# Half of a token's expert rows added by TensorE through diagonal weights, with the shared expert's down product in the same PSUM banks

## The chip, the core and the metric

The kernel runs on one core of one Trainium2 chip. The metric is the time of one execution on the device, in microseconds (us). The core has five engines that run their own instruction streams and meet at semaphores: TensorE (PE in the profile, its weight loads PEld), VectorE (DVE), ScalarE (ACT), GpSimd (POOL) and SyncE (SP). Transfers are issued by SyncE, ScalarE and GpSimd and run on 16 shared DMA engines.

## The reference, cut to what matters

The whole block is an adaptive norm, sparse attention and an RWKV7 branch side by side, their mix added to `x`, and then a mixture of experts. The change touches what follows the experts. With `T` = 512 tokens, `D` = 1024, 64 experts of width 256 and 8 experts for each token:

```
h2 = rms_norm(x, norm2_g) * (1 + sc2) + sh2
y[t] = sum over the 8 chosen experts e of  gw[t, e] * swiglu(h2[t], exp_gate[e], exp_up[e], exp_down[e])
shared = swiglu(h2, sh_gate, sh_up, sh_down)
x = x + g2 * (y + shared)
out = rms_norm(x, final_g)          # x * rsqrt(mean(x * x) + 1e-6) * final_g
```

All of it is float32.

## The kernel before

Tokens lie in four blocks `b` of 128 (one for each partition), so `x[b]` is a 128x1024 tile. The program has these stages, by the times of the profiled execution: the norms, attention and RWKV7 until about 680; the second norm, the router and the shared expert until about 808; the routed experts until about 1311; the end until 1388.

The shared expert. `shared_load` (L993) loads its weights, and GpSimd multiplies the down weights `shd` by `g2`. `shared_up` (L1006) makes `act`, the 256x512 product of gate and up. `shared_down` (L1020) is called for each block: two halves of 512 columns, two products each (`pssd`, L1027), and VectorE adds the result to `x[b]` (L1028).

The lists. `lists` (L1154) and `table` (L1177) turn the routing into a list of tokens for each expert: VectorE makes 32 one-hot masks `oh` (L1186), TensorE sums them against the tokens into `pstab` (L1188), VectorE copies that out (L1193) and forms rows `lr` (L1197), TensorE turns them (`psidx`, L1198) and VectorE casts them to the indices `idx` (L1199). `token_weights` (L1201) makes the weights `wk` of a token's eight rows. In this part a scheduler interleaves the instructions of the calls.

The routed experts. 50 slots of one expert each pass through six weight buffers `W[0]` to `W[5]` (3 MB each; `load_slot`, L1228, on SyncE's queue). Their tokens are worked in chunks of 64 rows: GpSimd gathers the rows (`gather`, L1241), VectorE transposes them (`hT`, L1252), `gate_up` (L1255) makes the product `pg`, ScalarE and VectorE make `sg` and `t` from it (L1269, L1271), `turn` (L1274) transposes `t`, and `down` (L1283) multiplies with the down weights; the result `o` is scaled by `g2` and stored in the DRAM tensor `od`, one row for each token and expert. This order is written out by hand. Slot 5's buffer lies where the lists and the shared expert's tiles were, so its load waits for them.

The end. `finish_begin` (L1388) makes 12 places for rows out of the buffers `W[1]` and `W[2]`, and puts `final_g` and two output tiles `ys` into `W[3]`. `finish` (L1399) is the branch that runs when no expert has more rows than its slot holds. For each block GpSimd gathers eight rows of 1024 for each token from `od` (L1406), VectorE adds each with its weight to `x[b]` (L1408), ScalarE sums the squares (L1411), VectorE takes the mean (L1412) and the reciprocal root in nine small steps (`rsqrt`, L143 to L155), scales (L1414), and SyncE stores the block (L1415). The scheduler mixes the blocks.

Of the kernel before, what the change touches and what calls it, by code (L numbers as in the profile page):

```python
# [19 lines left out]
P = 128  # L20
# [17 lines left out]
FILL = (3, 2)  # L38

# [123 lines left out]
class Block:  # L163
# [829 lines left out]
    def shared_load(self):  # L993
# [25 lines left out]

    def shared_down(self, b, pool, tag, bufs):  # L1020

        nc = self.nc
# [365 lines left out]
    def finish_begin(self):  # L1388

        flat = []  # L1390
        for j in (1, 2, 3):
            gu, d = self.W[j]
            gu = gu.rearrange("p j k f -> p (j k f)")
            flat.append([gu[:, D * m:D * m + D] for m in range(4)] + [d[:, m] for m in range(2)])
        self.rows = flat[0] + flat[1]
        self.fg, self.ys = flat[2][0], flat[2][1:3]
        self.nc.sync.dma_start(self.fg, self.ins["final_g"].rearrange("(o d) -> o d", o=1).to_broadcast([P, D]))

    def finish(self, od):  # L1399

        nc, fp, fg = self.nc, self.ep, self.fg
        for b in range(NB):
            x = self.x[b]
            for k in range(8):
                row = self.rows[(8 * b + k) % len(self.rows)]
                nc.gpsimd.indirect_dma_start(out=row, out_offset=None, in_=od,  # L1406
                                             in_offset=bass.IndirectOffsetOnAxis(ap=self.at[:, 8 * b + k:8 * b + k + 1], axis=0))
                nc.vector.scalar_tensor_tensor(x, row, self.wk[:, b, k:k + 1], x, op0=ALU.mult, op1=ALU.add)  # L1408
            y = self.ys[b % 2]
            ss, m, r = (fp.tile([P, 1], F32, tag=nm, name=nm, bufs=2) for nm in ("ss3", "m3", "r3"))  # L1410
            nc.scalar.activation(y, x, AF.Square, accum_out=ss)  # L1411
            nc.vector.tensor_scalar(m, ss, 1.0 / D, 1e-6, op0=ALU.mult, op1=ALU.add)  # L1412
# [129 lines left out]
```

## Time and profile before

| | us |
|---|---|
| time before, median of 3 runs | 1378.23 |
| lowest, highest | 1373.99, 1381.51 |
| the profiled execution | 1390.25 |
| its span | 1388.0 |
| TensorE, VectorE, ScalarE, GpSimd busy | 1192.2, 741.5, 304.2, 499.1 |

The mean granted clock of TensorE was 0.923 in the profiled execution. The span runs from the first to the last instruction or transfer of the execution; the rows further down are all taken from it, with times from its start. A shape such as 128x512 is partitions by elements. One float32 matmul call shows as two passes, so `shared_down`'s 16 calls are 32 instructions. "Idle before" is how long the engine stood before an instruction, and the arrow names what it was released by.

### The profile page before, as it was taken

How to read it: one execution, taken by the hardware profiler on the slowest of the kernel's cores; microseconds unless marked ns; L12 is line 12 of the kernel's file. 1: busy time of each engine (PE TensorE's matmuls, PEld its weight loads, DVE VectorE, ACT ScalarE, POOL GpSimd, SP SyncE). 2: the span in 40 equal slices, each digit the busy share in tenths (PEclk: the TensorE clock that was granted, in tenths of full speed). 3: DMA queues.
4: the chain of work that ended last, by engine and by line, in shares of the span. 5: the costliest groups of instructions: out<-in, count | busy, mean ns of one | idle time of the engine just before them, and what ended most of it. 6: DMA issues, size and time to landing. Idle time of an engine off the chain costs nothing. (4 is left out here: it accounts for less than half of the span.)

```text
span 1388.0 us, 25689 instructions
## 1 busy us (share of the span) xinstructions
PE 1192.2 (86%) x10057; PEld 727.7 (52%) x10057; DVE 741.5 (53%) x1783; ACT 304.2 (22%) x700; POOL 499.1 (36%) x483
## 2 busy tenths in 40 slices
PE   4899888998888899978889969999999999999600
PEld 3566555666666665666768634444444444444200
DVE  5783258887798977655566822222222222222167
ACT  6432411111133476524312000000000000000000
POOL 1555424433244734253421143333233333331073
PEclk9899999988899999989899979999999999999755
DMA  9683564200025842364371776999899999999586
GB/s 312 202 257 64 99 174 98 51 29 29 28 76 159 252 122 77 113 229 160 107 254 46 304 302 210 346 413 412 316 379 397 396 389 399 401 406 412 206 294 251
DMA packets 149342, 318.29 MB, mean 229 GB/s; under 512 B 13839, under 2 KB 89322, under 8 KB 130396
## 3 DMA queue, kind: packets, MB, share of 16 engines
q1 hardware_dynamic: 109332, 241.64, 48.9%
q0 software_dynamic: 19584, 43.27, 9.4%
q10 hardware_dynamic: 20296, 31.65, 6.3%
q8 instruction: 81, 1.33, 0.4%
q14 instruction: 49, 0.40, 0.1%
HBM read 278.58 MB, written 41.08 MB: 230 GB/s over the span
## 5 line engine op out<-in xcount | busy, mean ns | idle before, releaser
L1265 PE MATMUL pg<-wgu,hT 128*64 128x256 f32 (+1 forms) x3424 | 331.5, 397 | 17.4 <-DVE hT L1252 6.9
L1245 POOL DMA_INDIRECT G<-h2d,idx x160 | 151.3, 946 | 320.5 <-DVE hT L1252 271.7
L1265 PEld LDWEIGHTS pg<-wgu,hT 128*64 128x64 f32 (+1 forms) x3424 | 171.3, 123 | 171.4 <-issue 71.0
L1271 DVE TENSOR_TENSOR t<-sg,pg 128x128 f32<-128x128 f32 x80 | 23.0, 287 | 324.3 <-ACT sg L1269 324.3
L344 POOL TENSOR_TENSOR wl<-w,wh 128x512 fp32r<-128x512 f32 (+1 forms) x94 | 129.0, 1386 | 150.2 <-ACT wh L343 148.2
L182 PE MATMUL psz<-hh,wh 128*128 128x512 f32 (+1 forms) x352 | 150.2, 427 | 6.6 <-ACT wh L343 6.6
L1292 PE MATMUL pd<-wd,a 128*64 128x512 f32 (+1 forms) x856 | 153.8, 600 | 2.0 <-ACT a L1280 2.0
L183 PE MATMUL psz<-hl,wh 128*128 128x512 f32 (+1 forms) x352 | 150.1, 426 | 0.0
L184 PE MATMUL psz<-hh,wl 128*128 128x512 f32 (+1 forms) x352 | 147.6, 419 | 1.2 <-POOL wl L344 1.2
L343 ACT CAST wh<-w 128x512 fp32r<-128x512 f32 (+1 forms) x94 | 55.7, 611 | 140.3 <-PE psz L183 104.1
L182 PEld LDWEIGHTS psz<-hh,wh 128*128 128x128 f32 (+1 forms) x352 | 69.8, 198 | 28.4 <-issue 7.1
L1280 ACT COPY a<-psa 128x128 f32<-128x128 f32 x80 | 21.2, 265 | 281.5 <-PE psa L1278 154.8
L1294 DVE TENSOR_TENSOR o<-pd,g2h 128x512 f32<-128x512 f32 x80 | 55.3, 692 | 47.1 <-PE pd L1292 45.4
L183 PEld LDWEIGHTS psz<-hl,wh 128*128 128x128 f32 (+1 forms) x352 | 69.8, 198 | 17.4 <-issue 4.2
L1292 PEld LDWEIGHTS pd<-wd,a 128*64 128x64 f32 (+1 forms) x856 | 39.4, 122 | 74.3 <-issue 66.7
L184 PEld LDWEIGHTS psz<-hh,wl 128*128 128x128 f32 (+1 forms) x352 | 69.3, 197 | 17.2 <-POOL wl L344 2.1
L1269 ACT ACTIVATE sg<-pg 128x128 f32<-128x128 f32 x80 | 22.2, 277 | 174.4 <-PE pg L1265 158.7
L1252 DVE STREAM_TRANSPOSE hT<-G 128x512 f32<-128x512 f32 x80 | 56.3, 704 | 3.6 <-DMA G<-h2d,idx 3.6
L579 DVE STREAM_TRANSPOSE bdx<-X 32x128 f32<-32x128 f32 x160 | 48.3, 302 | 2.9
L239 DVE SCALAR_TENSOR_TENSOR acc<-adaw,sc,acc 128x1024 f32<-128x1024 f32 x28 | 44.1, 1576 | 9.9 <-DMA adaw<-in_ada_w_dram 9.4
L1406 POOL DMA_INDIRECT wgu<-od,rowat x22 | 23.7, 1079 | 68.4 <-issue 65.1
L779 DVE SCALAR_TENSOR_TENSOR acc<-rel,iw,acc 128x256 f32<-128x256 f32 (+2 forms) x45 | 38.1, 846 | 10.4 <-ACT rel L774 7.8
(414 smaller groups left out, 1872.7 us busy)
## 6 DMA issues: line engine op xcount, KB each, us to landing
wgu<-in_exp_gate_dram SPq DMA_DIRECT2D x50, 1024.0 KB
wgu<-in_exp_up_dram SPq DMA_DIRECT2D x50, 1024.0 KB
wd<-in_exp_down_dram SPq DMA_DIRECT2D x50, 1024.0 KB
adaw<-in_ada_w_dram SPq DMA_DIRECT2D x48, 512.0 KB
w<-in_w_in_dram SPq DMA_DIRECT2D x46, 512.0 KB
od<-o ACTq DMA_DIRECT2D x160, 128.0 KB
x<-in_x_dram SPq DMA_DIRECT2D x8, 512.0 KB
zg<-zst ACTq DMA_DIRECT2D x16, 256.0 KB
```

The lines of the kernel that those rows point to most:

```text
L182: nc.tensor.matmul(ps, ah, bh, start=first, stop=False)
L183: nc.tensor.matmul(ps, ah, bl, start=False, stop=False)
L184: nc.tensor.matmul(ps, al, bh, start=False, stop=last)
L239: nc.vector.scalar_tensor_tensor(acc, w, self.sc[:, k:k + 1], acc, op0=ALU.mult, op1=ALU.add)
L343: nc.scalar.copy(wh[:, ks, :n], w[:, ks, :n])
L344: nc.gpsimd.tensor_sub(wl[:, ks, :n], w[:, ks, :n], wh[:, ks, :n].bitcast(F32))
L579: nc.vector.transpose(bdx[z, :, z], X[z])
L1245: self.nc.gpsimd.indirect_dma_start(out=G[:, x], out_offset=None, in_=self.h2d.rearrange("t (q c) -> (t q) c", q=4), in_offset=bass.Indire ...
L1252: self.nc.vector.transpose(hT.rearrange("p k (s i) -> p s k i", i=32), G.rearrange("p s (k i) -> p s k i", i=32))
L1265: nc.tensor.matmul(pg[at:at + n], hT[:, k, n * x:n * x + n], ws[x][0][:, :, k, m::2], start=k == 0, stop=k == 7, tile_position=(0, at))
L1292: nc.tensor.matmul(pd[at:at + n], a[:, k, n * x:n * x + n], ws[x][1][:, k, T * h:T * h + T], start=k == 0, stop=k == 1, tile_position=(0, at))
L1294: nc.vector.tensor_mul(o, pd, self.g2h)
```

## The change

1. `shared_down` goes. The scaled `shd` is stored to DRAM (`shd_d`) on GpSimd's queue as soon as it is made, and `act` (`act_d`) on ScalarE's queue after `shared_up`. `finish_begin` loads both again, into `W[2]`, on SyncE's queue behind the last slot's load.
2. There are 28 places for rows instead of 12, in `W[4]`, `W[5]`, part of `W[3]`, `W[0]` and `W[1]`.
3. Of a block's eight rows, VectorE adds the first four to `x[b]`. The last four are added by TensorE: for each there is a 128x128 diagonal matrix `dg` of the token weights (16 in all, made by ScalarE during the last chunks, in `W[3]`), and `dg` times the row is accumulated in PSUM. The same two PSUM banks of a block get `act` times `shd` (the shared down product) and the identity times `x[b]`, so that they hold the whole sum.
4. Square and scale read PSUM, in two halves of 512 columns; the two sums of squares are added by one small step more. The output is stored in eight halves.
5. The order of the end is written out by hand (`manual_schedule`).

The core of the diff:

```diff
@@ shared_load
+        nc.gpsimd.dma_start(self.shd_d, self.shd)
@@ shared_down
-    def shared_down(self, b, pool, tag, bufs):
-        for hf in range(2):
-            ds = slice(hf * T, hf * T + T)
-            ps = pool.tile([P, T], F32, tag=tag, name="pssd", bufs=bufs)
-            for k in range(2):
-                nc.tensor.matmul(ps, self.act[:, k, b * P:(b + 1) * P], self.shd[:, k, ds], start=k == 0, stop=k == 1)
-            nc.vector.tensor_add(self.x[b][:, ds], self.x[b][:, ds], ps)
@@ finish_begin
-        self.rows = flat[0] + flat[1]
+        self.rows = flat[4] + flat[5] + flat[3][2:] + flat[0] + flat[1]
+        self.act, self.shd = flat[2][3].rearrange("p (k t) -> p k t", k=2), self.W[2][1]
+        self.dg = [flat[3][j // 8][:, P * (j % 8):P * (j % 8) + P] for j in range(NB * PEROWS)]
+        nc.sync.dma_start(self.shd, self.shd_d)
+        nc.sync.dma_start(self.act, self.act_d)
+        for b in range(NB):
+            for j in range(PEROWS):
+                nc.scalar.activation(self.dg[PEROWS * b + j], self.ident, AF.Copy, scale=self.wk[:, b, 8 - PEROWS + j:9 - PEROWS + j])
@@ finish
+        def shared(b):
+            sums[b] = [self.ps.tile([P, T], F32, tag=t, bufs=3, name="pssd") for t in ("pg", "pd")]
+            for h, hs in enumerate(halves):
+                for k in range(2):
+                    nc.tensor.matmul(sums[b][h], self.act[:, k, b * P:(b + 1) * P], self.shd[:, k, hs], start=k == 0, stop=False)
+        def last(b):
+            for h, hs in enumerate(halves):
+                nc.scalar.activation(y[:, hs], sums[b][h], AF.Square, accum_out=ss[:, h:h + 1])
+            nc.vector.tensor_add(m, ss[:, 0:1], ss[:, 1:2])
+            nc.vector.tensor_scalar(m, m, 1.0 / D, 1e-6, op0=ALU.mult, op1=ALU.add)
+            rsqrt(nc, fp, m, r, 1, "r3u")
+            for h, hs in enumerate(halves):
+                nc.vector.scalar_tensor_tensor(y[:, hs], sums[b][h], r, fg[:, hs], op0=ALU.mult, op1=ALU.mult)
+                nc.sync.dma_start(self.out[0, b * P:(b + 1) * P, hs], y[:, hs])
+        with self.tc.manual_schedule():
+            for b in range(NB):
+                for k in range(8): nc.gpsimd.indirect_dma_start(out=place(b, k), ...)
+                if b == 0:
+                    for c in range(NB - 1): shared(c)
+                for k in range(n):
+                    add(b, k)
+                    if b and k == 1: last(b - 1)
+                if b == NB - 1: shared(b)
+                for h, hs in enumerate(halves):
+                    nc.tensor.matmul(sums[b][h], self.ident, self.x[b][:, hs], start=False, stop=False)
+                for j in range(PEROWS):
+                    for h, hs in enumerate(halves):
+                        nc.tensor.matmul(sums[b][h], self.dg[PEROWS * b + j], place(b, n + j)[:, hs], start=False, stop=j == PEROWS - 1)
+            last(NB - 1)
@@ build
         self.shared_up(1, self.ps, "pd", 3)
+        nc.scalar.dma_start(self.act_d, self.act)
         self.load_slot(4)
         self.lists()
-        for b in range(NB):
-            self.shared_down(b, self.ps, "pd", 3)
         self.token_weights()
```

How the instructions stand in a row shows at three places. The first is TensorE just before the experts: `pstab` is the one-hot product, `psidx` the turning of the index rows, `pg` the first chunk's gate and up product. Before:

```order
L1188 MATMUL pstab<-tok,oh 60x64
L1027 MATMUL pssd<-shd,act 128x512
L1188 LDWEIGHTS oh
L1188 MATMUL pstab<-tok,oh 128x64
L1188 LDWEIGHTS oh
L1188 MATMUL pstab<-tok,oh 60x64
L1027 MATMUL pssd<-shd,act 128x512 x3
L1198 MATMUL psidx_7763<-idl,lr 128x128
L1027 MATMUL pssd<-shd,act 128x512
L1198 MATMUL psidx_7763<-idl,lr 128x60
L1027 MATMUL pssd<-shd,act 128x512 x3
L1265 MATMUL pg<-wgu_7450,hT 64x256 x20
```

After (lines 1181, 1191, 1258, 1271 are 1188, 1198, 1265, 1278 of before):

```order
L1181 MATMUL pstab<-tok,oh 60x64
L1181 LDWEIGHTS oh
L1181 MATMUL pstab<-tok,oh 128x64
L1181 LDWEIGHTS oh
L1181 MATMUL pstab<-tok,oh 60x64
L1191 MATMUL psidx_7769<-idl,lr 128x128
L1191 MATMUL psidx_7769<-idl,lr 128x60
L1258 MATMUL pg<-wgu_7455,hT 64x256 x20
L1271 MATMUL psa<-idl,t 128x128
```

The `pssd` products between the one-hot products, between the two `psidx` and behind them are gone, and nothing takes their place.

The second is VectorE in the end; `x_6852` and `x_6960` are the sums of blocks 1 and 2, `m` and `r` the mean and the root of block 0. Before:

```order
L1408 SCALAR_TENSOR_TENSOR x_6852<-wgu_7454,wk,x_6852 128x1024 x2
L1412 TENSOR_SCALAR m_12853<-ss_12852 128x1
L146 TENSOR_SCALAR r3u<-m_12853 128x1
L147 TENSOR_SCALAR r_12854<-r3u 128x1
L1408 SCALAR_TENSOR_TENSOR x_6852<-wd_7455,wk,x_6852 128x1024
L151 SCALAR_TENSOR_TENSOR r3u<-r_12854,m_12853 128x1
L152 SCALAR_TENSOR_TENSOR r_12854<-r3u,r_12854 128x1
L151 SCALAR_TENSOR_TENSOR r3u<-r_12854,m_12853 128x1
L1408 SCALAR_TENSOR_TENSOR x_6852<-wd_7455,wk,x_6852 128x1024
L152 SCALAR_TENSOR_TENSOR r_12854<-r3u,r_12854 128x1
```

After, where `x_6856` and `x_6965` are the sums of blocks 1 and 2; ahead of this piece stand four adds of block 0, two of block 1, the two steps for the mean of block 0 and the root's other steps:

```order
L157 TENSOR_TENSOR r_12882<-r_12882,r3u 128x1
L1427 SCALAR_TENSOR_TENSOR wgu_7459<-pssd,r_12882,wgu_7459 128x512 x2
L1415 SCALAR_TENSOR_TENSOR x_6856<-wd_7814,wk,x_6856 128x1024 x2
L1415 SCALAR_TENSOR_TENSOR x_6965<-wgu_7455,wk,x_6965 128x1024 x2
L1423 TENSOR_TENSOR m_12924<-ss_12923 128x1
L1424 TENSOR_SCALAR m_12924<-m_12924 128x1
```

The steps of a block's root stood between the adds of the next block; now root and scale stand in one piece between the first two and the last two adds of the next block, and the scale reads `pssd`, the sums in PSUM.

The third is TensorE in the end, which had no instruction there before: its last one was the `pd` product of the last chunk. After (L1412 the shared down product, L1445 the identity product, whose weights are `idl`, L1448 the diagonals):

```order
L1412 MATMUL pssd<-wd_7460,wgu_7459 128x512 x12
L1445 MATMUL pssd<-x_6854,idl 128x512 x2
L1448 MATMUL pssd<-wd_6439,wgu_7461 128x512 x4
L1448 MATMUL pssd<-wgu_7813,wgu_7461 128x512 x4
L1445 MATMUL pssd<-x_6856,idl 128x512 x2
L1448 MATMUL pssd<-wgu_7461 128x512 x4
L1448 MATMUL pssd<-wd_7462,wgu_7461 128x512 x4
L1445 MATMUL pssd<-x_6965,idl 128x512 x2
L1448 MATMUL pssd<-wd_7456,wgu_7461 128x512 x4
L1448 MATMUL pssd<-wgu_7457,wgu_7461 128x512 x4
L1412 MATMUL pssd<-wd_7460,wgu_7459 128x512 x4
L1445 MATMUL pssd<-x_7098,idl 128x512 x2
```

TensorE's instructions there are new: twelve calls for blocks 0 to 2 ahead, then two with `x[b]` and eight with rows for each block, and block 3's four shared ones after block 2.

## Rows read from the trace of the kernel before

**Rows 1.** Windows: us, PE, PEld, DVE, ACT, POOL busy (instructions), granted clock, DMA share, GB/s.

```profile
900.00:1286.00 386.00, 385.25 (x3583) 177.59 (x3581) 103.36 (x195) 35.26 (x130) 114.72 (x122) 1.00 0.99 393
...
1300.00:1311.00 11.00, 9.00 (x45) 3.43 (x42) 0.98 (x2) 0.81 (x3) 0.00 (x0) 0.81 0.21 61
```

**Rows 2.** Chain of waits before the experts: start, us, what ran or was waited for.

```profile
784.16 1.01 PE pstab L1188 x8
785.17 1.91 PE pssd L1027 x4
...
788.10 1.06 PE pssd L1027 x2
...
801.47 2.77 PE pssd L1027 x6
...
809.30 15.67 another core or an unknown queue
```

**Rows 3.** Groups by shape, 784 to 812: busy, mean ns | idle before, releasers.

```profile
L1027 PE MATMUL pssd<-shd,act 128*128 128x512 f32 x32 | 16.5, 625 | 0.0
L1186 DVE TENSOR_SCALAR oh<-iotab,blk 128x188 bf16<-128x188 bf16 x28 | 7.3, 274 | 3.2 <-PE pstab L1188 3.1
...
L1028 DVE TENSOR_TENSOR x<-x,pssd 128x512 f32<-128x512 f32 x8 | 5.5, 682 | 2.5 <-PE pssd L1027 2.5
```

**Rows 4.** Timeline, 803 to 834: start, us, engine, instruction, [idle before <- releaser].

```profile
805.02 1.09 POOL L1245 DMA_INDIRECT G<-h2d,idx  x1 [18.89 <-DVE lr L1197]
...
812.47 0.71 DVE L1252 STREAM_TRANSPOSE hT<-G 128x512 f32<-128x512 f32 x1 [3.56 <-DMA G<-h2d,idx]
...
813.29 6.07 PE L1265 MATMUL pg<-wgu,hT 128*64 128x256 f32 x32 [5.10 <-issue]
...
824.99 0.28 ACT L1269 ACTIVATE sg<-pg 128x128 f32<-128x128 f32 x1 [15.69 <-remote]
...
826.26 1.98 PE L1265 MATMUL pg<-wgu,hT 128*64 128x256 f32 x8 [6.90 <-DVE hT L1252]
```

**Rows 5.** Groups by shape in the end, 1311 to 1388.

```profile
L1408 DVE SCALAR_TENSOR_TENSOR x<-wgu,wk,x 128x1024 f32<-128x1024 f32 x22 | 28.1, 1282 | 14.2 <-DMA wgu<-od,rowat 14.1
...
L1411 ACT ACTIVATE wgu<-x 128x1024 f32<-128x1024 f32 x4 | 4.2, 1056 | 65.7 <-DVE x L1408 65.7
```

**Rows 6.** Windows in the end, columns as in rows 1.

```profile
1350.00:1370.00 20.00, 0.00 (x0) 0.00 (x0) 19.38 (x33) 2.30 (x4) 13.27 (x13) 0.50 1.02 411
```

**Rows 7.** Timeline of VectorE in the end, first rows.

```profile
1328.24 1.28 DVE L1408 SCALAR_TENSOR_TENSOR x<-wgu,wk,x 128x1024 f32<-128x1024 f32 x1 [0.66 <-DMA wgu<-od,rowat]
...
1336.94 2.50 DVE L1408 SCALAR_TENSOR_TENSOR x<-wgu,wk,x 128x1024 f32<-128x1024 f32 x2 [0.92 <-DMA wgu<-od,rowat]
```

**Rows 8.** Timeline of VectorE in the end, last block.

```profile
1375.04 2.61 DVE L1408 SCALAR_TENSOR_TENSOR x<-wgu,wk,x 128x1024 f32<-128x1024 f32 x2
1378.91 0.15 DVE L1412 TENSOR_SCALAR m<-ss 128x1 f32<-128x1 f32 x1 [1.26 <-ACT wgu L1411]
...
1381.01 1.29 DVE L1414 SCALAR_TENSOR_TENSOR wgu<-x,r,wgu 128x1024 f32<-128x1024 f32 x1
```

**Rows 9.** Timeline of VectorE before the experts.

```profile
785.63 0.80 DVE L1186 TENSOR_SCALAR oh<-iotab,blk 128x188 bf16<-128x188 bf16 x4
...
801.51 0.35 DVE L1193 COPY ls<-pstab 128x64 f32<-128x64 f32 x2 [0.60 <-PE pstab L1188]
```

**Rows 10.** Windows at the start of the experts, columns as in rows 1.

```profile
815.00:820.00 5.00, 4.36 (x26) 2.44 (x22) 0.00 (x0) 0.00 (x0) 3.78 (x4) 0.69 1.01 396
820.00:825.00 5.00, 0.00 (x0) 0.00 (x0) 0.00 (x0) 0.01 (x1) 1.89 (x2) 0.65 0.66 247
```

**Rows 11.** Windows of the stage ahead, columns as in rows 1.

```profile
725.00:745.00 20.00, 18.22 (x89) 15.62 (x90) 15.50 (x56) 3.18 (x9) 4.29 (x3) 0.91 0.07 27
```

**Rows 12.** Timeline of TensorE, start of the experts.

```profile
828.58 4.40 PE L1265 MATMUL pg<-wgu,hT 128*64 128x256 f32 x24
...
835.78 2.94 PE L1265 MATMUL pg<-wgu,hT 128*64 128x256 f32 x24
```

More of the change, by code (lines that the diff above doesn't have):

```diff
@@ L38 @@
 FILL = (3, 2)
+PEROWS = 4
 def _order():
@@ L1388, in finish_begin @@
     def finish_begin(self):
[L1390 to L1391 removed]
+        nc = self.nc
+        flat = {}
+        for j in (0, 1, 2, 3, 4, 5):
             gu, d = self.W[j]
             gu = gu.rearrange("p j k f -> p (j k f)")
[L1394 to L1395 removed]
+            flat[j] = [gu[:, D * m:D * m + D] for m in range(4)] + [d[:, m] for m in range(2)]
+        self.rows = flat[4] + flat[5] + flat[3][2:] + flat[0] + flat[1]
@@ L1399, in finish @@
+        for b in range(NB):
+            for j in range(PEROWS):
+                nc.scalar.activation(self.dg[PEROWS * b + j], self.ident, AF.Copy, scale=self.wk[:, b, 8 - PEROWS + j:9 - PEROWS + j])
     def finish(self, od):
         nc, fp, fg = self.nc, self.ep, self.fg
-        for b in range(NB):
[L1403 to L1408, printed above, removed]
-            y = self.ys[b % 2]
-            ss, m, r = (fp.tile([P, 1], F32, tag=nm, name=nm, bufs=2) for nm in ("ss3", "m3", "r3"))
-            nc.scalar.activation(y, x, AF.Square, accum_out=ss)
-            nc.vector.tensor_scalar(m, ss, 1.0 / D, 1e-6, op0=ALU.mult, op1=ALU.add)
-            rsqrt(nc, fp, m, r, 1, "r3u")
-            nc.vector.scalar_tensor_tensor(y, x, r, fg, op0=ALU.mult, op1=ALU.mult)
-            nc.sync.dma_start(self.out[0, b * P:(b + 1) * P], y)
@@ new lines, in finish, with add @@
+        n = 8 - PEROWS
+        place = lambda b, k: self.rows[(8 * b + k) % len(self.rows)]
+        halves = [slice(0, T), slice(T, D)]
+        sums = {}
+        def shared(b):
[3 more added lines that the diff above has]
+                    nc.tensor.matmul(sums[b][h], self.act[:, k, b * P:(b + 1) * P], self.shd[:, k, hs], start=k == 0, stop=False)
+        def add(b, k):
+            nc.vector.scalar_tensor_tensor(self.x[b], place(b, k), self.wk[:, b, k:k + 1], self.x[b], op0=ALU.mult, op1=ALU.add)
@@ new lines, in finish @@
+        with self.tc.manual_schedule():
+            for b in range(NB):
+                for k in range(8):
+                    nc.gpsimd.indirect_dma_start(out=place(b, k), out_offset=None, in_=od,
+                                                 in_offset=bass.IndirectOffsetOnAxis(ap=self.at[:, 8 * b + k:8 * b + k + 1], axis=0))
+                if b == 0:
+                    for c in range(NB - 1):
+                        shared(c)
+                for k in range(n):
+                    add(b, k)
+                    if b and k == 1:
+                        last(b - 1)
+                if b == NB - 1:
+                    shared(b)
+                for h, hs in enumerate(halves):
[4 more added lines that the diff above has]
+            last(NB - 1)
```

9 lines of the change are left out of this document (6 added, 3 removed).

## The prediction

> **What bounds the kernel now.** I read the windows of the stages first, then the chain of waits of the stage that loses the shared down product, then the timelines of the end.
>
> In the expert stage TensorE is busy 385.25 of 386 us while the DMA engines are 0.99 busy [rows 1]: both are full, and weights are loaded as TensorE frees their buffers, so what starts the stage earlier moves all of it. Two places are open. The first is the stretch before the experts. Its chain runs on TensorE from 784.16 on: nine pieces of one-hot products (`pstab`, mostly 8 passes and 1.01), and between each two of them `pssd`, once 1.91 and seven times 1.05 [rows 2]. `pssd` is what the change takes away there: 32 passes and eight adds of 0.68 on VectorE [rows 3]. Behind it GpSimd gathers the first token rows from 805.02, they are transposed at 812.47, the first gate/up product runs from 813.29 to 819.36, but ScalarE has its result only at 824.99 (it waited 15.69, "remote"), and TensorE goes on at 826.26 [rows 4]. The 5.6 us behind 819.36 have no owner in the trace: the chain calls the whole wait "another core or an unknown queue" [rows 2].
>
> The second is the end, 1311 to 1388. GpSimd fetches eight rows of results for each token, VectorE adds them at 1.28 each, 32 times or 41 us; the norm is one Square of 1.06 for each block of 128 tokens [rows 5] and a scale of 1.29 [rows 8]. TensorE has nothing to do there, its granted clock is 0.50; from 1350 to 1370 the DMA engines are 1.02 busy and VectorE 19.38 of 20 [rows 6]. The first rows are waited for: the fourth add starts at 1328.24, the eighth at 1336.94 [rows 7]. The last adds end at 1377.6, and behind them come Square, mean, square root, scale and store [rows 8].
>
> **The front stage.** VectorE's last 28 masks for the one-hot products start at 785.63 and take 0.27 each [rows 3, 9], so without `pssd` they end at about 793.4. From the copy of the finished table (801.51 [rows 9]) to the first gather it took 3.5 us; one step of the token weights (0.68 [rows 3]) stands ahead of that copy now as well. 793.4 + 0.7 + 3.5 = 797.6, so the first gather comes 7.4 earlier; I take 7.5. The first product would then end at 812.
>
> What that is worth hangs on the ownerless 5.6 us. DMA is 1.01 busy from 815 to 820 and 0.66 from 820 to 825 [rows 10]: the loads into the six weight buffers run out there. (a) If the late release is tied to this, the start doesn't move forward; it moves back by the new store of `act` (0.5 MB), at the 396 GB/s of [rows 10] 1.3 us. (b) If the 5.6 us follow the product, the experts start 7.5 earlier. (c) If they vanish, 7.5 + 5.6 = 13.1 earlier. I take (a), because the queue runs empty and the release comes within a microsecond or two, and no instruction of TensorE ends there.
>
> The Trainium skill, page "DMA: Bandwidth & Descriptors", section "Queues, rings and completion order", says that a DMA's semaphore write lands only after every earlier write of that DMA engine, over its queues. That would tie small gathers to the weight loads ahead of them and speak for (a), +1.3 instead of -7.5; the first gather, 7.45 us from issue to transpose with the queues full [rows 4], shows no wait for the drain.
>
> Edits at nothing: the store of `shd` (1 MB) stands on GpSimd's queue behind its own two products, at 745 at the latest, where DMA is 0.07 busy [rows 11]; GpSimd's gathers are 50 us behind it. Without that cover it costs 2.5 us. Slot 5's load on SyncE's queue waits for the two stores now instead of for `pssd`; the transfers ahead of it fill the DMA engines all the same. The 16 diagonals are ScalarE operations of 128x128, at 0.28 like `sg` [rows 4] 4.5 us among the last chunks; ScalarE is busy 35.26 of 386 us there [rows 1], and one diagonal can delay one hand-over by its 0.28: 0 to 1 us. The reloads of `shd`, `act` (1.5 MB) follow the last weight load on SyncE's queue, and DMA is 0.21 busy from 1300 to 1311 [rows 1]. The 28 places take no wait away from the path: the waits of the last adds are for rows, not of GpSimd for places, and DMA is full [rows 6].
>
> **The end.** Removed: 16 of 32 row adds, 20.5 us of VectorE. Added on TensorE for each block: 2 calls with the identity and 8 with diagonals, two passes each, so 20 passes. Six passes of this shape took 2.77 and four 1.91 [rows 2], which is 0.43 a pass and 0.19 once: 8.8 us at full clock. Of the 16 `pssd` calls 12 run from 1311.5 on while rows are fetched, four between the bursts of blocks 2 and 3.
>
> What decides is VectorE's order, written by hand. Norm and scale of block b-1 stand ahead of the last two adds of block b. They wait for the sums of block b-1, that is for TensorE's whole burst; and the burst of block b starts with the identity products, which need the last add of block b. So bursts and VectorE's tails follow one another and do not overlap. Without its burst a period is: Square of the second half, which I put at 0.8 (a whole one, with its hand-over, held VectorE up for 1.26 [rows 8]; half of it is 0.63); mean and square root, 1378.91 to 1381.01 [rows 8], 2.1, and one small add more, 0.2; two half scales from PSUM, at the 0.68 of the adds from `pssd` [rows 3] 1.4; two adds 2.6 [rows 8]; hand-over to TensorE 0.1. That is 7.2 us, in which TensorE stands.
>
> TensorE's clock: 24 passes of gate and up take 2.94 at full clock [rows 12], so 32 take 3.9 to 4.0. After a stand of 6.9 us, 8 took 1.98 [rows 4] and the next 24 took 4.40 [rows 12], 2.4 more. The product at 813.29, after a stand of 5.1, took 6.07 for 32 [rows 4], 2.1 more. So a burst after 7.2 us loses 0 to 2.4; I take 2, and 1 for the last, whose stand the four `pssd` calls halve.
>
> Sum: the fourth add of block 0 ends at 1328.24 + 1.28 = 1329.5, its eighth row is there at 1336.94 [rows 7], and the last four passes need 1.9, at half clock 3.5: burst 0 ends at 1338.8 to 1340.4, I take 1340. Then 3 x 7.2 + 3 x 8.8 + 2 + 2 + 1 = 53: burst 3 ends at 1393. Square, mean, root and scales, 0.9 + 2.3 + 1.4 = 4.6: 1397.6. From the last scale (1381.01 + 1.29 [rows 8]) to the end of the span it was 5.7; 0.25 MB less in the last store, at 411 GB/s [rows 6], makes it 5.1: 1402.7, or +14.7 on the span of 1388.0. Bounds: no loss of clock and burst 0 early, +8; 2.4 lost each time, +17.
>
> The Trainium skill, page "TensorE: Matmul & The Clock Gate", section "Why this matters for your kernels", warns of idle gaps between bursts of matmuls, since the clock falls back in them. The rows agree and put it at 2 us a burst; if all of a burst ran at the low clock, the sum would be that of rival 4.
>
> **Time.** The profiled execution took 1390.25, the median is 1378.23; the differences of the profile are put on the median: 1378.2 + 14.7 + 1.3 = 1394.
>
> **Rivals.** 1: the end as above, front (b): 1378.2 + 14.7 - 7.5 = 1385.4 (1379 to 1388). For it: the first product runs at a granted clock of 0.69, so its true end may lie behind the modelled one; against it: 5.6 us are as much as the whole product. 2, not slower: the end as above, but the 5.6 us vanish, (c): 1379.8 (1373 to 1382). It decides if `sg` starts before 813. 3, faster or the same: the end is bound by the landing of rows, which is what a hidden TensorE would give: last row at about 1372 [rows 6, 8], then four passes 1.9, 4.6 and 5.1: span 1383.6, or -4.4; with (a) 1375, with (b) 1366, with (c) 1361. Against it: it needs periods of 11 us, where the order above gives 18. 4: bursts at half clock from end to end: 1340 + 3 x (7.2 + 17.4) is 21 more than the sum, 1415.
>
> **How the numbers follow.** Forecast 0.45 (1387 to 1397), rival 1 0.21, rival 2 0.16, rival 3 0.14, rival 4 0.04. Left out are rival 4, rival 3 with an earlier start and the low edge of rival 2; the range is 1376 to 1399. A measurement of this kernel tells about 0.5%, 6.9 us, from no change, so 1371.3 to 1385.1 is "same". Faster: rival 3 with (b) or (c) and a third of it with (a), 0.09. Same: its rest, rival 2 and half of rival 1, 0.31. Slower: 0.60.
>
> **What would show it.** The first gather at about 797.5; the first `sg` at 825 to 826 (forecast), 817 (rival 1) or 812 (rival 2). In the end VectorE waits three times, some 9 to 11 us, ahead of the small add of the two Square sums; TensorE waits some 7 us ahead of each pair of identity products; the last scale lies 86 us behind the last down product, not 71. The forecast is wrong if VectorE adds more than two rows of the next block beside a burst, or if a burst takes far from 9 to 11 us.

## The result and the profile after

The changed kernel took 1398.91 us (median of 4 runs, 1394.44 to 1403.1) beside 1379.87 (1373.99 to 1389.16) of the kernel before, a ratio of 1.0122 with an interval of 1.0078 to 1.0165. A second measurement of the same two, with 12 runs of the changed kernel and 35 of the one before, gave 1.0060 (1.0031 to 1.0089), medians 1394.97 and 1384.94. It is slower, by 0.6 to 1.2%; the second figure rests on more runs. The profiled execution took 1395.14, its span is 1393.3 against 1388.0 before.

Absolute times hide where the 5.3 us of the spans come from, because the stage before the experts began 4.9 us later in this execution. So I cut both traces at the same events: the first mask of the one-hot products, the start of the second chunk's gate/up product, the end of the last down product, the end of the span.

| us | before | after | difference |
|---|---|---|---|
| first mask starts at | 781.82 | 786.75 | +4.9 |
| front: first mask to second chunk's product | 44.44 | 32.74 | -11.7 |
| experts: to the end of the last down product | 485.11 | 481.51 | -3.6 |
| tail: to the end of the span | 76.62 | 92.33 | +15.7 |

The tail was forecast at +14.7. The front was forecast at +1.3 and came out at -11.7. The experts' 3.6 lies within the scatter of that stage, which took 480.5 to 485.6 in the profiles of this study.

**The front.** The timeline of the changed kernel (start, length, engine, line, operation, in square brackets the idle time before it and its releaser), which answers [rows 4] and the first of [rows 9]:

```profile
786.75 0.27 DVE L1179 TENSOR_SCALAR oh<-iotab,blk 128x188 bf16<-128x188 bf16 x1
...
790.56 8.66 DVE L1179 TENSOR_SCALAR oh<-iotab,blk 128x188 bf16<-128x188 bf16 x28
790.88 9.45 PE L1181 MATMUL pstab<-tok,oh 128*128 128x64 bf16 x56 [0.78 <-DVE oh L1179]
...
800.37 0.35 DVE L1186 COPY ls<-pstab 128x64 f32<-128x64 f32 x2 [0.54 <-PE pstab L1181]
...
802.97 1.61 POOL L1238 DMA_INDIRECT G<-h2d,idx  x1 [11.90 <-DVE idx L1192]
...
811.20 0.71 DVE L1245 STREAM_TRANSPOSE hT<-G 128x512 f32<-128x512 f32 x1 [6.69 <-DMA G<-h2d,idx]
...
812.12 6.06 PE L1258 MATMUL pg<-wgu,hT 128*64 128x256 f32 x32 [8.69 <-DVE hT L1245]
...
818.21 0.28 ACT L1262 ACTIVATE sg<-pg 128x128 f32<-128x128 f32 x1 [13.34 <-PE pg L1258]
...
819.48 1.12 PE L1258 MATMUL pg<-wgu,hT 128*64 128x256 f32 x8 [1.31 <-DVE hT L1245]
```

The masks run without waits for TensorE now, 28 in 8.66. The first gather comes 16.22 behind the first mask, before it was 23.20. The product ends at 818.18 and `sg` starts at 818.21, released by TensorE: the ownerless 5.6 us are gone.

Windows of that stretch (window, its length, busy time of PE, PEld, DVE, ACT, POOL with the number of instructions, granted TensorE clock, DMA share, GB/s), which answer [rows 10]:

```profile
795.00:805.00 10.00, 6.13 (x33) 3.77 (x32) 7.88 (x32) 0.20 (x1) 1.73 (x2) 0.50 1.01 424
...
815.00:820.00 5.00, 3.69 (x26) 2.05 (x24) 0.91 (x2) 0.28 (x1) 3.78 (x5) 0.81 1.02 398
820.00:825.00 5.00, 5.00 (x39) 2.43 (x35) 0.91 (x2) 0.54 (x2) 2.81 (x3) 1.00 0.64 220
```

`sg` starts in the middle of a window in which the DMA engines are 1.02 busy. The load queue runs out later, as in the kernel before, and nothing waits for it.

**The end.** TensorE's timeline from the last down product on:

```profile
1297.70 3.29 PE L1285 MATMUL pd<-wd,a 128*64 128x512 f32 x8 [2.00 <-ACT a L1273]
1300.93 10.86 PE L1412 MATMUL pssd<-wd,wgu 128*128 128x512 f32 x24
1318.41 3.77 PE L1445 MATMUL pssd<-x,idl 128*128 128x512 f32 x4 [6.63 <-DVE x L1415]
1321.99 3.62 PE L1448 MATMUL pssd<-wd,wgu 128*128 128x512 f32 x8
1325.45 3.60 PE L1448 MATMUL pssd<-wgu,wgu 128*128 128x512 f32 x8
1336.86 3.78 PE L1445 MATMUL pssd<-x,idl 128*128 128x512 f32 x4 [7.81 <-DVE x L1415]
1340.44 4.63 PE L1448 MATMUL pssd<-wgu 128*128 128x512 f32 x8
1344.91 3.60 PE L1448 MATMUL pssd<-wd,wgu 128*128 128x512 f32 x8
1355.58 3.78 PE L1445 MATMUL pssd<-x,idl 128*128 128x512 f32 x4 [7.08 <-DVE x L1415]
1359.16 3.81 PE L1448 MATMUL pssd<-wd,wgu 128*128 128x512 f32 x8
1362.81 3.60 PE L1448 MATMUL pssd<-wgu,wgu 128*128 128x512 f32 x8
1366.24 3.60 PE L1412 MATMUL pssd<-wd,wgu 128*128 128x512 f32 x8
1373.43 3.56 PE L1445 MATMUL pssd<-x,idl 128*128 128x512 f32 x4 [3.60 <-DVE x L1415]
1376.83 7.03 PE L1448 MATMUL pssd<-wgu,wgu 128*128 128x512 f32 x16
```

Four bursts of 20 passes start 18.45, 18.72 and 17.85 apart, and TensorE stands 6.6 to 7.8 ahead of the first three. VectorE's timeline shows the other half of the alternation, the three waits ahead of the small add of the Square sums:

```profile
1349.26 0.21 DVE L1423 TENSOR_TENSOR m<-ss 128x1 f32<-128x1 f32 x1 [6.08 <-ACT wgu L1422]
...
1352.93 5.11 DVE L1415 SCALAR_TENSOR_TENSOR x<-wgu,wk,x 128x1024 f32<-128x1024 f32 x4
1367.16 0.16 DVE L1423 TENSOR_TENSOR m<-ss 128x1 f32<-128x1 f32 x1 [9.12 <-ACT wgu L1422]
...
1370.78 2.59 DVE L1415 SCALAR_TENSOR_TENSOR x<-wd,wk,x 128x1024 f32<-128x1024 f32 x2
1384.62 0.16 DVE L1423 TENSOR_TENSOR m<-ss 128x1 f32<-128x1 f32 x1 [11.24 <-ACT wgu L1422]
...
1386.91 1.41 DVE L1427 SCALAR_TENSOR_TENSOR wgu<-pssd,r,wgu 128x512 f32<-128x512 f32 x2
```

In the list of waits of the end (us in total, times, longest) the two sides weigh the same, each waiting for the other in turn:

```profile
DVE m L1423 <- ACT wgu L1422: 26.4, 3, 11.2
...
PE pssd L1445 <- DVE x L1415: 25.1, 4, 7.8
```

### The profile page after: what moved, and what is told of

Same layout as the page of the kernel before. It is cut to its first block, busy times and chain, and to the rows that moved or that the text cites. A ratio compares the mean times of both kernels' runs of the same rounds, so it can differ in the third digit from the quotient of the medians.

```text
span 1393.3 us, 25870 instructions
## 1 busy us (share of the span) xinstructions
PE 1233.9 (89%) x10137; PEld 743.6 (53%) x10137; DVE 719.8 (52%) x1767; ACT 310.4 (22%) x724; POOL 499.3 (36%) x484
## 5 line engine op out<-in xcount | busy, mean ns | idle before, releaser
L1258 PE MATMUL pg<-wgu,hT 128*64 128x256 f32 (+1 forms) x3424 | 326.5, 393 | 16.5 <-DVE hT L1245 10.0
L1258 PEld LDWEIGHTS pg<-wgu,hT 128*64 128x64 f32 (+1 forms) x3424 | 166.8, 122 | 170.3 <-issue 71.8
L184 PEld LDWEIGHTS psz<-hh,wh 128*128 128x128 f32 (+1 forms) x352 | 69.9, 198 | 28.1 <-issue 7.1
```

The costliest lines, as they stand in the source:

```text
L184: nc.tensor.matmul(ps, ah, bh, start=first, stop=False)
L1258: nc.tensor.matmul(pg[at:at + n], hT[:, k, n * x:n * x + n], ws[x][0][:, :, k, m::2], start=k == 0, stop=k == 7, tile_position=(0, at))
```

## Experiments

Ratios are to the kernel before on the same chip, with 95% intervals. Times of single profiles are used only within a stage, since executions of one kernel differ by several us in when the first mask starts (see "The sum").

**The kernel before, again.** No edit.

> The kernel before, unchanged, once more, for a second profile and for what two equal kernels differ by. My theory on its scatter: the 5.6 us between the end of the first gate/up product (819.36 in the first profile) and ScalarE's sg (824.99) are not there in every execution, and the first 300 us differ by some us from one execution to the next (the profile of the changed kernel lost 4.9 us there between 256 and 305 us, in code that the change doesn't touch). Then the span is anywhere from 1372 to 1388 and a stretch-by-stretch comparison shows which of the two it was. Rival: the 5.6 us are part of this kernel, and sg starts 5 to 6 us behind the product's end again. Ratio to the kernel before 1.000 within 0.005 either way.

0.9983 (0.9949 to 1.0017). Front 44.46, tail 78.28; before 44.44 and 76.62. So stage lengths repeat within 0.1 in the front and 1.7 in the tail.

**The front alone.** The changed kernel with the end of the kernel before; it leaves out the shared expert's down product.

```
 def finish(self, od):
-    (PSUM sums, diagonals, hand order)
+    for b in range(NB): 8 gathers, 8 adds, Square, scale, store (as before)
```

> The front half of the change alone: shared_down is taken out, shd and act are stored as in the changed kernel, but the end is that of the kernel before (12 places, all eight rows added by VectorE), and the shared expert's down product is left out of the result. Theory of the profile comparison: the first gather comes about 7 us earlier counted from the first one-hot mask, the experts start 8 to 13 us earlier and the whole time falls by as much: 1366 to 1372, ratio 0.990 to 0.995. Rival 1, my forecast (a): the start of the experts is tied to the drain of the weight loads, ratio 1.000 to 1.002. Rival 2: the gain at the start is given back within the expert stage, where DMA is the bound (DMA 1.00 from 900 to 1286 in the changed kernel, with waits for loads of 1.40 and 3.38 us at 1280 and 1289): experts start 8 to 13 earlier, but the last down product lies under 5 earlier, ratio 0.997 to 1.000.

0.9960 (0.9928 to 0.9992), front 34.33, tail 79.07. The front's gain is real, 10.1 us less than before in that stage. Over the whole kernel it is 0.4% or 5.5 us, fewer than the 8 to 13 expected; where the rest goes stands under "The sum" below.

**The end alone.** The kernel before with the new end, without the shared products and their reloads in it; `shared_down` stays where it was.

```
 sums[b] = [self.ps.tile(...) for t in ("pg", "pd")]
-(two shared products into each half)
...
-nc.tensor.matmul(sums[b][h], self.ident, self.x[b][:, hs], start=False, stop=False)
+nc.tensor.matmul(sums[b][h], self.ident, self.x[b][:, hs], start=True, stop=False)
```

> The end of the change alone: the front is that of the kernel before, with shared_down before the lists; the end is the changed one (28 places, four rows by TensorE through diagonals, the identity product, halves, order by hand), without the shared products and without the reloads of shd and act. Theory: bursts and VectorE's tails alternate, so the stretch from the last down product to the end of the span is 92 us as in the changed kernel (76.6 before), less about 3 for the four shared calls that no longer stand behind block 2's burst: those were hidden under VectorE's tail, so it stays 90 to 92; ratio to before 1.010 to 1.012. Rival: the shared products and their reloads are what lengthens the end; then the stretch is 77 to 82 and the ratio 1.000 to 1.004.

1.0100 (1.0063 to 1.0138), front 44.39, tail 91.62. The end's loss, 15.0 and 13.3 over the two tails of before, comes without any of the shared products, so it lies in the row sums.

**The hand order.** Norm and scale of block b-1 stand behind the last add of block b instead of ahead of its third.

```
-if b and k == 1:
+if b and k == n - 1:
     last(b - 1)
```

> The changed kernel with one number of its order by hand changed: norm and scale of block b-1 stand behind the fourth add of block b instead of behind the second. Theory: the adds that a burst waits for no longer wait for the burst before, so bursts follow one another within 0 to 1 us (burst 8.8 against VectorE's 9.6 in a period), the clock stays up, and the end is bound by the landing of the rows (about 60 us behind the last down product) and the last norm: stretch from the last down product to the end 72 to 78 instead of 92, ratio to before 0.998 to 1.003, that is 14 to 20 us under the changed kernel. Rival: TensorE's passes, the clock or the DMA set the end whatever VectorE's order; then the stretch stays above 88 and the ratio at 1.010 or more.

0.9937 (0.9902 to 0.9972), tail 77.81. One index takes back all that the end lost. TensorE's waits for VectorE's adds, from this kernel's list of waits of the end:

```profile
PE pssd L1445 <- DVE x L1415: 8.3, 2, 5.8
```

8.3 in two waits stand against 25.1 in four (one stand of 4.3 more is put down to TensorE's own issue). So the stands are 5.8, 4.3 and 2.4 ahead of the first three bursts and not the 0 to 1 expected, and the first four passes of each still take 3.3 to 3.8. The last burst follows the shared products of block 3 without a gap, where the changed kernel stood 3.60 (TensorE's timeline):

```profile
1359.16 3.60 PE L1412 MATMUL pssd<-wd,wgu 128*128 128x512 f32 x8
1362.59 1.88 PE L1445 MATMUL pssd<-x,idl 128*128 128x512 f32 x4
1364.31 7.03 PE L1448 MATMUL pssd<-wgu,wgu 128*128 128x512 f32 x16
```

**The changed kernel, again.** No edit.

> The changed kernel, unchanged, once more, beside the kernel before with more runs than the first comparison had (ratio 1.0122 from four runs each). By parts I expect less: the profiles put the start 10 to 11.7 us earlier (44.4 us from the first one-hot mask to the second chunk's product before, 32.7 to 34.5 without shared_down) and the end 14 to 15.7 us later (stretch from the last down product 76.6 to 79.1 before, 91.6 to 92.3 changed), which is +3 to +5 us, ratio 1.002 to 1.005. Rival: the first comparison is right, and 10 us or more lie in a part that the profiles of two kernels don't compare well, the first 400 us, whose length differs by up to 16 us between executions; ratio 1.008 or more.

1.0060 (1.0031 to 1.0089), front 32.91, tail 91.86: the two stages as in the first profile (32.74 and 92.33).

**The identity products last.** VectorE's sum joins a block's bank at the end of the burst instead of its start.

```
-for h, hs in enumerate(halves):
-    nc.tensor.matmul(sums[b][h], self.ident, self.x[b][:, hs], start=False, stop=False)
 for j in range(PEROWS):
     ...
+for h, hs in enumerate(halves):
+    nc.tensor.matmul(sums[b][h], self.ident, self.x[b][:, hs], start=False, stop=True)
```

> The changed kernel with the identity products (x[b]) moved behind the eight diagonal products of each block; VectorE's order stays. Theory: the chain through x[b] then holds only the last 4 of a burst's 20 passes (1.9 us), the other 16 run while VectorE works on the block before. A period falls from 18 to 7.2 + 1.9 + 1 = 10, below the pace at which rows land (about 11), so the stretch from the last down product to the end is 74 to 79 instead of 92; ratio to before 0.990 to 0.995. Rival: the low clock after each stand takes the gain, stretch over 84.

0.9938 (0.9908 to 0.9968), tail 76.03. VectorE's order is the old one; the burst no longer waits for it. TensorE's timeline:

```profile
1337.13 5.40 PE L1446 MATMUL pssd<-wgu 128*128 128x512 f32 x8 [3.04 <-DMA wgu<-od,rowat]
...
1349.10 3.70 PE L1446 MATMUL pssd<-wd,wgu 128*128 128x512 f32 x8 [1.42 <-DMA wd<-od,rowat]
...
1361.90 7.13 PE L1446 MATMUL pssd<-wgu,wgu 128*128 128x512 f32 x16 [0.52 <-DMA wgu<-od,rowat]
1368.87 1.88 PE L1448 MATMUL pssd<-x,idl 128*128 128x512 f32 x4
```

What it waits for now is the landing of rows, and its window in the middle of the end has the DMA engines full (0.99, at full clock):

```profile
1350.00:1365.00 15.00, 14.48 (x34) 6.19 (x33) 12.84 (x25) 1.38 (x4) 8.31 (x7) 1.00 0.99 376
```

**Both of these edits.**

> Both orders together: norm and scale of block b-1 behind the fourth add of block b, and identity products behind the diagonal ones. Theory: rows' landing binds with either, so both give no more than one: stretch from the last down product to the end 73 to 78, within 2 us of order_late (77.8) and of x_last; ratio 0.990 to 0.995. Rival: the bursts still bind in order_late and both together take another 5 us or more.

0.9941 (0.9908 to 0.9974), tail 77.67: not beyond either alone. Once the two engines overlap, the rows set the end, and the tail (76.0 to 77.8 in the three) is that of before (76.6 to 78.3): taking 16 of 32 adds off VectorE gains nothing there.

**A warm TensorE.** The changed kernel, with 26, 28, 28 and 12 unused 128x128 products ahead of the identity products of blocks 0 to 3.

```
+spare = self.ps.tile([P, P], F32, tag="rt", bufs=2, name="psa")
+for _ in range((26, 28, 28, 12)[b]):
+    nc.tensor.matmul(spare, self.ident, self.ident, start=True, stop=True)
```

> The changed kernel with products of the identity with itself, whose result nobody reads, put on TensorE ahead of each block's identity products (26, 28, 28, 12 calls of 128x128), so that it doesn't stand before a burst. They measure the clock's term. Theory: a burst of 20 passes falls from 10.4 to 11.5 us (in the profile of the changed kernel) to 8.8 to 9, and the stretch from the last down product to the end by 5 to 7 us, from 92 to 85 to 87; ratio to before 1.000 to 1.003 where the changed kernel has 1.002 to 1.008. Rival: the passes take longer for another reason (waits for rows, for VectorE, weight loads); then bursts stay above 10.

1.0005 (0.9970 to 1.0039), tail 88.76. The bursts still alternate with VectorE. Three of them take 8.9 now (the third 1348.60 to 1357.46, before 10.8); the second is as slow as it was, 11.9, because the first two adds of its block had waited for rows and TensorE stood 2.90 behind the spare products (TensorE's timeline):

```profile
1329.67 3.78 PE L1448 MATMUL pssd<-x,idl 128*128 128x512 f32 x4 [2.90 <-DVE x L1415]
1333.24 4.87 PE L1451 MATMUL pssd<-wgu 128*128 128x512 f32 x8
...
1348.60 1.98 PE L1448 MATMUL pssd<-x,idl 128*128 128x512 f32 x4 [0.81 <-DVE x L1415]
1350.42 3.60 PE L1451 MATMUL pssd<-wd,wgu 128*128 128x512 f32 x8
1353.86 3.60 PE L1451 MATMUL pssd<-wgu,wgu 128*128 128x512 f32 x8
```

With three of four bursts warm, the clock is worth 3.3 us of the tail (92.1, the mean of the two profiles of the changed kernel, to 88.76), fewer than the 5 to 7 expected; the 11 to 13 from there to the tails of the three kernels above are in the main the order's. The ratio is 0.55%, or 7.6 us, below the changed kernel's; the spare products can't account for all of it, since the first mask, far ahead of them, starts at 780.82 here and at 786.75 and 784.42 there (see "The sum").

**Is the ownerless stall the drain of the load queue?** The kernel before, with the last of the queued weight loads (slot 5) issued only behind the first chunk's product and held there by three one-column memsets.

```
 if c == 0:
+    nc.vector.memset(self.W[5][0][:, 0, 0, 0:1], 0.0)
+    ... (two more columns)
+    self.load_slot(5)
...
-self.load_slot(5)          (in build, ahead of the experts)
```

> The kernel before, with the load of slot 5's weights (3 MB) held back until the first chunk's t is made (three one-column memsets of its buffer by VectorE stand there, and the load waits for them). It asks what the 5.4 to 5.75 us between the end of the first gate/up product and sg belong to, which all three profiles with the old front have. Theory of my forecast, case (a): they end with the drain of the weight loads, sg came 1.4 to 1.7 us behind it; without slot 5's load the queue is empty before the product ends, and sg starts within 0.5 us of the product's end, the second chunk's product about 5 us earlier. Rival: they belong to the old front's work on TensorE or to its place in the program, and stay at 5 to 6.

One execution of each: 1389.1 beside 1389.83; front 44.42. The queue is nearly empty while the stall goes on as before; windows and the two ends of the stall:

```profile
815.00:820.00 5.00, 4.95 (x28) 2.78 (x24) 0.00 (x0) 0.00 (x0) 3.78 (x5) 0.62 0.36 111
820.00:825.00 5.00, 0.00 (x0) 0.00 (x0) 0.00 (x0) 0.00 (x0) 2.14 (x3) 0.72 0.29 89
```

```profile
813.75 6.20 PE L1265 MATMUL pg<-wgu,hT 128*64 128x256 f32 x32 [5.21 <-issue]
...
825.30 0.28 ACT L1269 ACTIVATE sg<-pg 128x128 f32<-128x128 f32 x1 [15.65 <-remote]
```

The product ends at 819.95 and `sg` starts 5.35 later with the DMA engines 0.29 busy. The drain is not what it waits for.

**TensorE's passes put back.** The front alone, with 16 products of `pssd`'s shape (identity times `x`, results unused, no adds) where `shared_down` was. The shared down product is left out of the result here too.

```
+def idle_down(self, b, pool, tag, bufs):
+    for hf in range(2):
+        ps = pool.tile([P, T], F32, tag=tag, name="pssd", bufs=bufs)
+        for k in range(2):
+            nc.tensor.matmul(ps, self.ident, self.x[b][:, ds], start=k == 0, stop=k == 1)
```

> front_alone (shared_down and its adds out, the shared expert's down product left out of the result) with 16 products of the same shape put back where shared_down stood, identity times x, that nobody reads; slot 5's load doesn't wait for them and VectorE adds nothing. It splits the front's gain. Theory: the stretch from the first one-hot mask to the second chunk's product has two parts, TensorE's order (31.5 us to the first product with shared_down, 25.4 without) and the stall behind the product (5.4 to 5.75, and 0 to 1.9). If TensorE's passes alone make the first part, it is 29 to 31.5 again. If the stall belongs to slot 5's late load, it stays at 0 to 2 here; rival: TensorE's passes bring it back to 5 or more.

One execution of each: 1395.09 beside 1389.83; front 43.53. The stall is back, 6.4 us from 824.30 to 830.69:

```profile
819.23 5.07 PE L1267 MATMUL pg<-wgu,hT 128*64 128x256 f32 x32 [4.43 <-issue]
...
830.69 0.28 ACT L1271 ACTIVATE sg<-pg 128x128 f32<-128x128 f32 x1 [18.68 <-remote]
```

The stores of `shd` and `act`, the missing adds and slot 5's other wait are all still in this kernel, so both parts of the front's gain come from taking TensorE's passes out.

**Fewer gathers in a row.** The kernel before, with four gather buffers instead of six and gathers three chunks ahead, so that 10 gathers follow one another on GpSimd ahead of the first product's release, not 14.

```
-G = self.gp.tile([P, 2, 256], F32, tag="G", name="G", bufs=6)
+G = self.gp.tile([P, 2, 256], F32, tag="G", name="G", bufs=4)
...
-for c in range(min(5, n)):
+for c in range(min(3, n)):
```

> The kernel before with four buffers for gathered rows instead of six, filled three chunks ahead instead of five, so that GpSimd issues ten gathers in a row at the start of the experts instead of fourteen. In all five profiles with the old front (shared_down or products of its shape in it) sg starts 19.9 to 20.0 us after the first gather, while the first gate/up product starts 8.3 to 8.5 and ends 13.6 to 14.6 after it. Theory: the release is tied to this row of gathers, the last of which is issued 17.4 us after the first; with four fewer, at 1.25 each, sg comes 5 us earlier, at 14.9 to 15.1, or at the product's end if that is later, and the stall is under 1. Rival: the gathers have nothing to do with it; sg stays 19.5 to 20.5 after the first gather and the stall at 5 to 6.

0.9935 (0.9898 to 0.9972), front 39.02. With all of `pssd` in place, the stall is gone:

```profile
803.23 1.09 POOL L1245 DMA_INDIRECT G<-h2d,idx  x1 [18.88 <-DVE lr L1197]
...
811.64 6.09 PE L1265 MATMUL pg<-wgu,hT 128*64 128x256 f32 x32 [5.25 <-issue]
...
817.77 0.28 ACT L1269 ACTIVATE sg<-pg 128x128 f32<-128x128 f32 x1 [10.27 <-PE pg L1265]
```

The product starts 8.41 behind the first gather, as in before (8.27), so the 5.4 us are the stall's alone.

**Identity last and fewer gathers.** Both edits in the changed kernel.

> x_last and gather_few together: the changed kernel with the identity products last, and gathers three chunks ahead into four buffers. x_last alone had ratio 0.9938 and no stall behind the first product (0.04), so theory: the fewer gathers have nothing left to give at the start, front 32 to 33 us as in x_last, stretch from the last down product to the end 75 to 78, ratio 0.990 to 0.995, the same as either alone within the interval. Rival: fewer gathers in flight help at other places too (the gathers share the DMA engines with the weight loads all through the expert stage), experts under 482 us and ratio under 0.990.

0.9908 (0.9874 to 0.9942), 1380.41 beside 1395.02: front 32.62, tail 78.44. It has the lowest ratio of all versions, though its interval overlaps those of the three orders above and of fewer gathers, and it is faster than both kernels. The identity products last take the end back to before; the front's gain is what remains.

## Why the prediction was right in time and wrong in one stage

**What bounds, the end's order: right.** The prediction said that norm and scale ahead of the last two adds make bursts and VectorE's tails follow one another. The waits of both sides show it (26.4 and 25.1), and an index (hand order) or a swap (identity last), each alone, undoes it.

**The period: right, term by term.** Stand of TensorE between bursts 7.2 forecast; 7.8, 7.1 and, with the four `pssd` calls inside it, 7.0 measured (the 6.6 ahead of the first burst is a wait for the first rows). Burst 8.8 forecast at full clock, 8.9 measured in the warm kernel; loss of clock 2, 2, 1 forecast. The four bursts took 10.6, 11.6, 10.8 and 10.4, that is 1.6 to 2.8 over 8.8, the last included. That one was mis-sized: the four `pssd` calls ahead of it shorten its stand to 3.60, and it lost 1.6 all the same, not 1. From the end of the last down product to the end of burst 0 I had 1340 - 1311.4 = 28.6; it was 28.1, but by another sum, so that this agreement is luck: I had the landing of the eighth row and four passes behind it, and no pass of burst 0 waited for a row; what made it are 17.4 to the end of the fourth add and a burst of 10.6. VectorE's waits were put at 9 to 11 and were 6.1, 9.1 and 11.2: the first is short because the adds of block 2 ahead of it had themselves waited 3.33 and 0.47 for rows. The last scale lies 85.9 behind the last down product, forecast 86. Rival 3 fell, and so did rival 4: a burst returns to full clock inside itself, as its last eight passes show, 3.60 in the first three. The warm kernel agrees with the section of the Trainium skill, page "TensorE: Matmul & The Clock Gate", that the prediction weighed: idle gaps cost, here 1.6 to 2.8 us a burst. But the gaps were made by the order, and undoing it gave back more than the clock's price.

**The front, first gather: right.** 16.2 behind the first mask, from 23.2: 7.0 earlier, forecast 7.5. Without `pssd` TensorE is busy 6.13 of the 10 us from 795 to 805 at a granted clock of 0.50, the lower of its two levels (1.2 GHz); in before it is busy all 10 there at 1.00 (2.4 GHz). Its last 56 one-hot passes took 9.45 without a pause, 0.17 each, where eight took 1.01 [rows 2], 0.13 each, and the copy of the table waited for them until 800.37, 1.15 behind the last mask. I had left no time for that; in return copy to gather took 2.60, not 3.5. The first product came only 6.1 earlier: it took 9.15 from first gather to product instead of 8.27. That part isn't TensorE's. Of the 0.88, 0.52 are the issue of the first gather on GpSimd (1.61 instead of 1.09), 0.27 the stretch from the second gather to the transpose and 0.10 that from the transpose to the product. The first issue takes 1.6 in all eight profiles without `pssd`'s passes and 1.1 in the six with them; why, no run shows.

**The front, the ownerless 5.6 us: wrong.** The step that failed is choice (a), "if the late release is tied to this, the start doesn't move forward". I took it because queue and release ended within a microsecond or two of each other. In the changed kernel `sg` starts with the DMA engines 1.02 busy, and with slot 5 late the stall lasts 5.35 on a nearly empty queue (0.29). What came is (c): 6.1 plus the vanished 5.6, -11.7, rated at 0.16. (Set back by the 4.9 of the later first mask, `sg` starts at 813.3, near the 812 of rival 2.) So the page "DMA: Bandwidth & Descriptors" of the Trainium skill, section "Queues, rings and completion order", which I had weighed in favour of (a), bears on no wait here: the one semaphore that `sg` waits for is TensorE's, not a DMA's, and the trace does not show the rule at work in this place.

**What then did the stall hang on?** In all five profiles with `pssd` and the full row of gathers, `sg` starts 19.9 to 20.0 behind the first gather (before 19.97, again 19.98, end alone 19.91, slot 5 late 19.92, passes put back 19.97), whatever the product did. With ten gathers in the row it starts 14.5 behind, with the product. That ties the stall to the row of gathers. But the changed fronts with six buffers issue 14 and more gathers in a row too, and `sg` starts 14.7 to 16.9 behind the first; two of them (hand order and front alone, 1.9 and 1.6) keep a rest of the stall. So the row of gathers is a condition that the runs show; why it stands in the way with `pssd` ahead of it and hardly without, no run shows, and it stays open.

The traces narrow it. `sg` waits for one semaphore, which TensorE updates, and in before the update itself comes 19.94 behind the first gather, 0.03 ahead of `sg`. So ScalarE isn't late: the 5.6 lie between the end of TensorE's last pass, which the profile models, and TensorE's update, and whether the passes ended later than modelled can't be told. Late instructions are not seen either: in none of the five profiles does a packet of the two DMA queues that the profile lists as instruction queues run during the stall. One rival is left untested, the recording itself. Each gather's landing makes 16 updates; from 8 to 25 us behind the first gather the traces hold 37 to 52 such updates in the five profiles with the stall, 59 and 64 in the two with a rest of it, 82 and 101 in the two with four buffers, and 238 to 242 in the five others. So records are lost in every profile with a late update, but also in two without one; whether the recording has a part in the wait, no run tells.

**The sum.** With -11.7 instead of +1.3 and the tail as forecast, the time should have been that of rival 2, some 1380. It was 1395 to 1399, near the forecast of 1394, for two reasons that the prediction did not have. One is the base: the forecast adds to 1378.2, and the kernel before had medians of 1379.87 and 1384.94 beside the changed one. As a difference the forecast +16 is the +17 of the first measurement and twice the +8 of the second. The other is the first mask. It started at 775.1 to 786.9 (mean 781.2) in the five profiles with `shared_down` and the old route (before, again, end alone, slot 5 late, fewer gathers) and at 780.8 to 789.9 (mean 785.8) in the nine without, 4.6 later.

The largest piece of the scatter arises between 250 and 305 us, in which both kernels issue the same instructions in the same order. The same passes of TensorE lie 0.7 earlier in the first profile of the changed kernel than in that of before at 250, and 6.1 later at 305. There TensorE runs at a lower granted clock and gets through fewer passes (windows, columns as in rows 1; before, then changed):

```profile
250.00:310.00 60.00, 53.90 (x1021) 37.77 (x1021) 52.82 (x180) 10.01 (x30) 20.59 (x26) 0.94 0.15 39
```

```profile
250.00:310.00 60.00, 52.44 (x925) 37.85 (x924) 46.29 (x152) 8.96 (x27) 19.26 (x24) 0.86 0.14 39
```

Both profiles of before have 0.94 there and both of the changed kernel 0.86. The step of 5.4 to 6.9 us goes with that clock in every profile: end alone and slot 5 late, which keep `shared_down`, have it too (0.86), as have the others without `shared_down` (0.86 to 0.89), while fewer gathers and the warm kernel lack it (0.97). So it isn't the work that the change moves; why the clock falls there in some of these kernels and not in others, no run shows.

Taken as real, the parts add up to the second measurement: front -11.5 to -11.7, tail +13.5 to +15.7, start +4.6 give +6 to +9, where +8 was measured; the +17 of the first, from four runs each, lies outside. Front alone: -10.1 + 4.6 = -5.5 against a measured 0.4% or 5.5; the hand order -10 + 0 + 4.6 = -5.4 against 0.6% or 8.7. But the starts spread by 12 among the five, also by other stretches than this one, so how much of the 4.6 a kernel has on average stays open. The forecast time was right by luck in part: two misses, -13 in the front and about +5 ahead of it, cancelled in part, and the base lay higher than the forecast's.

## What to carry to other kernels

In an order written by hand, ask of each wait what stands behind it on its engine: two adds behind a wait for TensorE made two engines take turns and cost 14 us, and one index or a reordered accumulation gave it all back. Give the operand that comes last the last place in an accumulation. A wait without an owner that ends near another event need not be tied to it; move the other event before building a term on it, and compare stage lengths, since whole spans of equal kernels differ by more than the effect. Compare the granted clock of the stages that a change leaves alone, too: here it moved the start by more than half of what the change won at the front.

## What the runs showed of the hardware

- A row of 14 indirect gathers on GpSimd goes with a hand-over from TensorE to ScalarE that is 5.35 to 6.4 us late, always 19.9 to 20.0 behind the first gather, where `pssd`'s passes run ahead of it; with 10 gathers the hand-over takes 0.04. The late piece is TensorE's own semaphore update; the cause is open.
- Passes taken off TensorE lowered the clock of those that stayed: granted 0.50 from 795 to 805 without the shared passes, 1.00 with them; a one-hot pass took 0.17 instead of 0.13.
- A burst of 20 passes of 128x512 takes 8.9 us warm, 10.4 to 11.6 after a stand of 3.6 to 7.8 and 11.9 after one of 2.9; the loss falls in its first four to twelve passes (3.78 for the first four, 1.98 warm; the last eight take 3.60 either way).
- The start of one and the same stage, 780 us into the program, scatters by 15 us over the executions of these kernels (775.1 to 789.9); 5.4 to 6.9 of that go with a lower granted clock of TensorE between 250 and 310 us (0.86 to 0.89 in ten profiles, 0.94 to 0.97 in four), while the front of one kernel repeats within 0.2 and its tail within 1.7.
